# Two of eight channel blocks of a causal depthwise convolution on ScalarE and GpSimd, inside a decoder layer on one core

## The chip, the cores and the metric

One core of a Trainium2 chip runs the whole program. The metric is the device time of one execution in microseconds, as the median of several runs. Engines are named as in the profile: PE is TensorE, DVE is VectorE, ACT is ScalarE, POOL is GpSimd, SP is SyncE, which issues nearly all DMAs.

## The reference

One decoder layer for 256 tokens of width 2048, in float32. A matrix product with `w_in` gives columns for a convolution group and for an attention group. The part that matters here is the convolution group, with 1024 channels and 31 taps:

```python
a, g = jnp.split(conv_in, 2, axis=-1)
u = a * jax.nn.sigmoid(g)
u = causal_depthwise_conv(u, conv_w[l], conv_b[l])
u = jax.nn.silu(layernorm(u, conv_ln_g[l], conv_ln_b[l]))
```

The attention group (low-rank queries, keys and values, rotary key, causal softmax) runs between the convolution's input and the place where its result is used: both groups meet in the product with `w_out`. A SwiGLU feed-forward block of width 5632 follows, which is the larger part of the time and is not touched.

## The kernel before, in words

Every large matrix product is done in float16 with a split of both operands into an upper and a lower half: three matmuls on TensorE for one (lines 147 to 155). The weights come as float32 blocks of 128 x 2048 (four tiles of 128 x 512, or of 128 x 448 for the latent weights) through four stage buffers. `Weights.load` (L124) issues the DMA on SP's queue (L136), and `split` (L107) then makes the upper half on ScalarE (L108) and the lower half on VectorE (L109). The feed-forward weights go the same way through `Feed.split` (L690). There are eight buffers for each half, so the split can run ahead of TensorE by up to eight blocks.

The convolution works with channels in partitions: `upad` holds 8 channel blocks of 128 channels, each with 30 zeros and 256 tokens, and `cacc` the 8 sums of 128 x 256. The loop over `j` (L303) goes over four groups of `w_in` columns. Each gives two channel blocks, called a quarter: a matrix product, the GLU (tanh L312 and a scaled copy L314 on ScalarE, a product L316 on VectorE), a transpose on TensorE (L319) and a copy into `upad` (L320).

Each quarter puts 31 taps into the list `conv_todo`, and `pump(n)` takes the next n off it, in order. A tap of a quarter is one of three kinds (`conv_tap`, L279):

- tap 0: two ScalarE activations that write `cacc` with the bias (L284);
- a tap whose number is not a multiple of 4: two VectorE instructions of 128 x 256, one for each block, that multiply and add into `cacc` (L289);
- taps 4, 8, ..., 28: two ScalarE products into a buffer (L295), and one VectorE addition of 128 x 512 for both blocks (L297). The buffer is the space of `x_sb`, in 8 slots of 512 columns.

So a quarter is 46 instructions of L289 and 7 of L297 on VectorE, and 16 activations. The numbers in `PUMPS` (L36) say how many taps are given out at which place: after each of the four column groups, after each of the three groups of latent weights (`lat`, L365), after the rotary queries (`uqp`, L412), in the value projection (`v`, L422) and in each of the eight attention heads (`head`, L509). What is left would come before the LayerNorm (`ln_mean`, L528, called in the first part of the `w_out` product). The compiler's scheduler orders each engine's instructions by their place in the program and by when it takes them to be ready; on the chip each engine then runs its instructions in that order.

GpSimd has little to do: the power in the RMS norms (L207), and in each head a scaling of the probabilities (L481) and a sum of squares (L498, L500). The rope key (L374 to L386) is turned on VectorE (its last step is the copy L384) and transposed on TensorE (L385), in front of the rotary query products in TensorE's order.

Of the kernel before, what the change touches and what calls it, by code (L numbers as in the profile page):

```python
# [13 lines left out]
AF = mybir.ActivationFunctionType  # L14
ALU = mybir.AluOpType
# [3 lines left out]
S = 256  # L19
NTB = 2  # L20
D = 2048
KD = D // P
C = 1024
CB = C // P
TAPS = 31
# [6 lines left out]
KL = 512  # L32
FF = 5632
KF = FF // P
ACT_NUM, ACT_DEN = 1, 4
PUMPS = dict(conv=(3, 8, 13, 14), lat=(11, 16, 9), v=(1, 0), uqp=3, head=(2, 7, 4, 8, 4, 4, 9, 8))  # L36
NG = 22


# [9 lines left out]
W_S = 128.0  # L49
# [11 lines left out]
def hymba_layer(ctx: ExitStack, tc: tile.TileContext, x, xT, pos, inv_freq, g_pre, w_in, w_lat,  # L61
                q_norm, w_uqn, w_uqp, kv_norm, w_uk, w_uv, conv_w, conv_v, g_attn,
                w_out, g_post, g_ffn, w_gu, w_dn, g_ffo, out):
    nc = tc.nc
# [14 lines left out]
    def region(kb, shape, dtype=F32):  # L79

        n = int(np.prod(shape)) * (2 if dtype == F16 else 4) // 4
        a = int(kb * KB)
        v = arena[:, a : a + n]
        if dtype != F32:
            v = v.bitcast(dtype)
        names = "abcd"[: len(shape)]
        if len(shape) > 1:
            v = v.rearrange(f"p ({' '.join(names)}) -> p {' '.join(names)}", **dict(zip(names[:-1], shape[:-1])))
        return v
# [3 lines left out]
    def nm(base):  # L93
        uid[0] += 1
        return f"{base}_{uid[0]}"

    def acc_tile():
        return ps_acc.tile([P, 512], F32, tag="acc", name=nm("acc"))

    def tmp_tile():  # L100
        return ps_tmp.tile([P, 512], F32, tag="tmp", name=nm("tmp"))
# [5 lines left out]
    def split(hi, lo, src, scale):  # L107
        nc.scalar.activation(hi, src, AF.Copy, scale=scale)  # L108
        nc.vector.scalar_tensor_tensor(lo, src, scale, hi, op0=ALU.mult, op1=ALU.subtract)  # L109
# [6 lines left out]
    class Weights:  # L116
# [4 lines left out]
            self.kpb = max(1, 2048 // n)  # L121
            self.parts = []

        def load(self, src, scale, first=None, before=None):  # L124

            n = self.n
            per = self.kpb
            k0 = 0
            pieces = list(first or [])
            while k0 < self.kt:  # L130
                kk = pieces.pop(0) if pieces else per
                kk = min(kk, self.kt - k0)
                st = stage.tile([P, 2048], F32, tag="stage", name=nm("st"))
                if before is not None:
                    before(k0, k0 + kk)
                nc.sync.dma_start(st[:, : kk * n], src[:, k0 * n : (k0 + kk) * n])  # L136
                for j in range(0, kk, self.kpb):
                    w = min(self.kpb, kk - j) * n
                    hi = wsp.tile([P, 2048], F16, tag="whi", name=nm("whi"))
                    lo = wsp.tile([P, 2048], F16, tag="wlo", name=nm("wlo"))  # L140
                    split(hi[:, :w], lo[:, :w], st[:, j * n : j * n + w], scale)
                    for i in range(min(self.kpb, kk - j)):
                        self.parts.append((hi[:, i * n : (i + 1) * n], lo[:, i * n : (i + 1) * n]))
                k0 += kk
            return self

    def mm3(ps, x_of, wgt, tbs=(0, 1), k0=0, start=True, stop=True):

        for k in range(wgt.kt):
            wh, wl = wgt.parts[k]  # L150
            for p_ap, tb in zip(ps, tbs):
                xh, xl = x_of(k0 + k, tb)
                nc.tensor.matmul(p_ap, xh, wh, start=(start and k == 0), stop=False)  # L153
                nc.tensor.matmul(p_ap, xh, wl, start=False, stop=False)  # L154
                nc.tensor.matmul(p_ap, xl, wh, start=False, stop=(stop and k == wgt.kt - 1))  # L155
# [10 lines left out]
    def flat(h, l):  # L166

        return lambda k, tb: (h[:, k, TB[tb]], l[:, k, TB[tb]])
# [9 lines left out]
    x_sb = const.tile([P, NTB, D], F32, name="x_sb")  # L178
# [40 lines left out]
    wg1 = Weights(KD, 512).load(w_in[1], W_S, before=load_tokens)  # L219
# [4 lines left out]
    cw = region(26.5, (CB, TAPS))  # L224
    nc.sync.dma_start(cw, conv_w)
    cv = const.tile([P, 4, CB], F32, name="cv")
# [44 lines left out]
    upad = region(52, (CB, PAD + S))  # L271
    nc.gpsimd.memset(upad[:, :, 0:PAD], 0.0)
    cacc = region(61, (CB, S))

    conv_todo = []
    prod = x_sb.rearrange("p t (a c s) -> p (t a) c s", a=4, c=2)
    prod_n = [0]

    def conv_tap(quarter, k):  # L279

        cbs = range(2 * quarter, 2 * quarter + 2)
        if k == 0:
            for cb in cbs:
                nc.scalar.activation(cacc[:, cb, :], upad[:, cb, 0:S], AF.Identity, scale=cw[:, cb, 0:1],  # L284
                                     bias=cv[:, 0, cb : cb + 1])
            return
        if k % ACT_DEN >= ACT_NUM:
            for cb in cbs:
                nc.vector.scalar_tensor_tensor(cacc[:, cb, :], upad[:, cb, k : k + S], cw[:, cb, k : k + 1],  # L289
                                               cacc[:, cb, :], op0=ALU.mult, op1=ALU.add)  # L290
            return
        t = prod[:, prod_n[0] % 8]
        prod_n[0] += 1
        for i, cb in enumerate(cbs):
            nc.scalar.activation(t[:, i, :], upad[:, cb, k : k + S], AF.Copy, scale=cw[:, cb, k : k + 1])  # L295
        a = cacc[:, cbs[0] : cbs[-1] + 1, :]
        nc.vector.tensor_tensor(a, a, t, op=ALU.add)  # L297

    def pump(n):
        for _ in range(min(n, len(conv_todo))):  # L300
            conv_tap(*conv_todo.pop(0))

    for j in range(4):  # L303
        if j == 0:
            ps = ps0
        else:
            wgt = wg1 if j == 1 else Weights(KD, 512).load(w_in[j], W_S)
            ps = [acc_tile(), acc_tile()]
            mm3(ps, h_of, wgt)
        for tb in range(NTB):  # L310
            th = work.tile([P, 256], F32, tag="A", name=nm("th"), bufs=3)
            nc.scalar.activation(th, ps[tb][:, 256:512], AF.Tanh, scale=r_half[:, tb : tb + 1])  # L312
            av = work.tile([P, 256], F32, tag="B", name=nm("av"), bufs=3)
            nc.scalar.activation(av, ps[tb][:, 0:256], AF.Copy, scale=r_half[:, tb : tb + 1])  # L314
            u = work.tile([P, 256], F32, tag="C", name=nm("u"), bufs=2)
            nc.vector.scalar_tensor_tensor(u, th, 1.0, av, op0=ALU.add, op1=ALU.mult)  # L316
            tp = tmp_tile()
            for i in range(2):
                nc.tensor.transpose(tp[:, i * P : (i + 1) * P], u[:, i * P : (i + 1) * P], ident)  # L319
            nc.scalar.copy(upad[:, 2 * j : 2 * j + 2, PAD + tb * P : PAD + (tb + 1) * P],  # L320
                           tp[:, : 2 * P].rearrange("p (c t) -> p c t", c=2))
        conv_todo += [(j, k) for k in range(TAPS)]
        pump(PUMPS["conv"][j])


# [13 lines left out]
    def latent_norm(z, gb, n, hl, dst):  # L339
        for tb in range(NTB):  # L340
            ss = smalls()
            nc.scalar.activation(junk_tile(n), z[:, tb, :], AF.Square, accum_out=ss)
            r = rstd_of(ss, n)
            nc.vector.scalar_tensor_tensor(z[:, tb, :], z[:, tb, :], r, gb, op0=ALU.mult, op1=ALU.mult)
            split(hl[:, tb, 0, :], hl[:, tb, 1, :], z[:, tb, :], X_S)
            nc.sync.dma_start_transpose(dst.rearrange("p a k t -> p (a k) t")[:, :, TB[tb]],
                                        hl[:, tb].rearrange("p a n -> p (a n)"))
# [9 lines left out]
    for j in range(3):  # L357
        wgt = Weights(KD, LN).load(w_lat[j], W_S)
# [4 lines left out]
        if j == 1:  # L363
            latent_norm(z_q, g_q, QL, q_hl, qn)
        pump(PUMPS["lat"][j])  # L365

# [23 lines left out]
    wgt = Weights(QL // P, 512).load(w_uqp, W_S)  # L390
    ps = [acc_tile(), acc_tile()]
    mm3(ps, lat_of(qn), wgt)
    for tb in range(NTB):
# [17 lines left out]
        nc.scalar.copy(qpT[:, :, TB[tb]], tp.rearrange("p (i t) -> p i t", i=H // 2))  # L411
    pump(PUMPS["uqp"])  # L412


    v_sb = region(44, (NTB, H * P))
    for j in range(2):
        wgt = Weights(KL // P, 512).load(w_uv[j], W_S)
        ps = [acc_tile(), acc_tile()]
        mm3(ps, lat_of(kvn), wgt)
        for tb in range(NTB):  # L420
            nc.scalar.activation(v_sb[:, tb, j * 512 : (j + 1) * 512], ps[tb], AF.Copy, scale=U)
        pump(PUMPS["v"][j])  # L422

# [81 lines left out]
    for h in range(H):  # L505
        ss = scores(h)
        if h + 2 < H:
            project(h + 2)
        pump(PUMPS["head"][h])  # L509
        attend(h, ss)  # L510
# [54 lines left out]
    for j in range(4):  # L565
        wgt = Weights(CB, 512).load(w_out[4 + j], W_S)
        ps = [acc_tile(), acc_tile()]
        mm3(ps, flat(mx_h[:, CB:], mx_l[:, CB:]), wgt)
        for tb in range(NTB):
            nc.scalar.activation(mix[:, tb, j * 512 : (j + 1) * 512], ps[tb], AF.Copy, scale=r_a[:, tb : tb + 1])  # L570
        if j == 0:
            pump(len(conv_todo))
            ln_mean()
        elif j == 1:
            ln_var()
        elif j == 2:
            conv_norm()
            for tb in range(NTB):
                nc.sync.dma_start(x_sb[:, tb, :], x[:, tb, :])
# [408 lines left out]
```

## Time and profile before

| | us |
|---|---|
| median of 3 runs | 1000.91 |
| lowest and highest run | 1000.34, 1001.33 |
| the profiled execution's own time | 1001.55 |
| its span in the profile | 999.7 |
| TensorE busy in the span | 959.6 |
| VectorE busy | 876.3 |
| ScalarE busy | 578.1 |
| GpSimd busy | 33.6 |
| granted TensorE clock, share of full speed | 0.994 |

All views are of the profiled execution, whose time is its span and what lies around it. A busy share is the time in which at least one instruction of the engine runs; neighbouring instructions overlap by some 0.08 us, so the time that one takes of its engine's queue is read from the starts of a dense run. The convolution and the attention lie in the first 290 us.

### The profile page before, as it was taken

The numbers are of one execution on the slowest core, as the hardware profiler recorded it, in microseconds if no ns is written. First come the engines' busy times: TensorE is split into PE (matmuls) and PEld (weight loads), VectorE is DVE, ScalarE is ACT, GpSimd is POOL, SyncE is SP. The second block draws the span as 40 slices with busy tenths as digits, with TensorE's granted clock in tenths as the row PEclk, the third lists the DMA queues.
The fourth block names the chain that finished last, engine by engine and source line by source line (L and its number), as shares of the span: only waits on it lengthen the run. The fifth ranks groups of instructions, "written<-read, shape, count | busy, mean of one in ns | idle before, by whom it ended". The sixth has DMA issues, their size and how long they took to land.

```text
span 999.7 us, 11980 instructions
## 1 busy us (share of the span) xinstructions
PE 959.6 (96%) x4577; PEld 454.4 (45%) x4577; DVE 876.3 (88%) x1024; ACT 578.1 (58%) x632; POOL 33.6 (3%) x50
## 2 busy tenths in 40 slices
PE   6999997999899998999999999999999999999995
PEld 2444553775444443444444444444444444444442
DVE  6799999999967999989898997897996988899855
ACT  7796764664666555655656645654663565555521
POOL 0000000033100100000000000000000000000000
PEclk9999998999999999999999999999999999999998
DMA  8974656476654966776875874784686646645532
GB/s 340 346 262 126 243 197 192 154 247 211 211 210 118 325 167 197 256 278 197 320 214 178 317 236 155 272 288 156 220 309 234 218 185 246 238 175 220 210 127 85
DMA packets 84010, 221.95 MB, mean 222 GB/s; under 512 B 55792, under 2 KB 56432, under 8 KB 61424
## 3 DMA queue, kind: packets, MB, share of 16 engines
q1 hardware_dynamic: 83232, 220.26, 63.7%
q10 hardware_dynamic: 720, 0.93, 0.3%
q8 instruction: 36, 0.59, 0.2%
q14 instruction: 22, 0.18, 0.1%
HBM read 204.25 MB, written 4.19 MB: 209 GB/s over the span
## 4 chain that ended last, share of the span: by engine, by line
PE 60%; DVE 23%; issue 5%; ACT 4%; DMA 3%; POOL 1%; SPq 0%; DVEq 0%; POOLq 0%; ACTq 0%
PE acc L740 10%; PE acc L741 10%; PE acc L739 10%; PE tmp L741 6%; PE tmp L740 6%; PE tmp L739 6%; DVE wlo L695 6%; DVE arena L289 3%; DVE wlo L109 3%; DVE st L709 2%; PE acc L155 2%; PE acc L153 2%; PE acc L154 2%; DMA st<-in_w_gu 2%; POOL sm L207 1%
## 5 line engine op out<-in xcount | busy, mean ns | idle before, releaser
L694 ACT ACTIVATE whi<-st 128x2048 f16<-128x2048 f32 (+1 forms) x177 | 317.1, 1798 | 228.7 <-PE acc L741 77.6
L695 DVE SCALAR_TENSOR_TENSOR wlo<-st,whi 128x2048 f16<-128x2048 f32 (+1 forms) x177 | 375.2, 2150 | 52.9 <-ACT whi L694 52.5
L740 PE MATMUL acc<-wlo,arena 128*128 128x512 f16 x620 | 235.0, 379 | 4.7 <-DVE wlo L695 4.7
L739 PE MATMUL acc<-whi,arena 128*128 128x512 f16 x620 | 235.0, 379 | 2.5 <-DVE q L773 1.4
L741 PE MATMUL acc<-whi,arena 128*128 128x512 f16 x620 | 235.0, 379 | 0.0
L153 PE MATMUL acc<-whi,arena 128*128 128x512 f16 (+1 forms) x380 | 143.5, 378 | 5.5 <-ACT whi L108 5.5
L741 PEld LDWEIGHTS <-arena 128*128 128x128 f16 x951 | 93.0, 98 | 117.4 <-issue 5.6
L154 PE MATMUL acc<-wlo,arena 128*128 128x512 f16 (+1 forms) x380 | 143.4, 377 | 2.2 <-DVE wlo L109 2.0
L740 PEld LDWEIGHTS <-arena 128*128 128x128 f16 x951 | 93.0, 98 | 114.3 <-issue 2.4
L739 PEld LDWEIGHTS <-arena 128*128 128x128 f16 x951 | 93.0, 98 | 113.3 <-DVE a L796 1.2
L155 PE MATMUL acc<-whi,arena 128*128 128x512 f16 (+1 forms) x380 | 143.3, 378 | 0.0
L739 PE MATMUL tmp<-whi,arena 128*128 128x512 f16 x331 | 125.4, 379 | 0.0
L740 PE MATMUL tmp<-wlo,arena 128*128 128x512 f16 x331 | 125.4, 379 | 0.0
L741 PE MATMUL tmp<-whi,arena 128*128 128x512 f16 x331 | 125.4, 379 | 0.0
L109 DVE SCALAR_TENSOR_TENSOR wlo<-st,whi 128x2048 f16<-128x2048 f32 (+4 forms) x59 | 118.2, 2009 | 6.5 <-ACT whi L108 6.5
L709 DVE TENSOR_TENSOR st<-st 128x1024 f32<-128x1024 f32 x135 | 117.2, 868 | 4.1
L108 ACT ACTIVATE whi<-st 128x2048 f16<-128x2048 f32 (+4 forms) x59 | 98.5, 1677 | 34.4 <-PE acc L155 10.3
L289 DVE SCALAR_TENSOR_TENSOR arena<-arena 128x256 f32<-128x256 f32 x184 | 78.5, 488 | 0.0
L153 PEld LDWEIGHTS <-arena 128*128 128x128 f16 x380 | 37.8, 99 | 47.4 <-ACT arena L113 5.0
L155 PEld LDWEIGHTS <-arena 128*128 128x128 f16 x380 | 37.8, 99 | 44.8 <-issue 5.1
L154 PEld LDWEIGHTS <-arena 128*128 128x128 f16 x380 | 37.6, 99 | 42.3 <-issue 2.8
L295 ACT ACTIVATE x_sb<-arena 128x256 f32<-128x256 f32 x56 | 25.3, 506 | 10.1 <-DVE arena L297 10.1
(209 smaller groups left out, 667.9 us busy)
## 6 DMA issues: line engine op xcount, KB each, us to landing
st<-in_w_gu SPq DMA_DIRECT2D x88, 1024.0 KB, 5.5
st<-in_w_dn SPq DMA_DIRECT2D x44, 1024.0 KB, 5.0
st<-in_w_out SPq DMA_DIRECT2D x16, 1024.0 KB, 5.1
st<-in_w_in SPq DMA_DIRECT2D x14, 1024.0 KB, 9.2
st<-in_w_lat SPq DMA_DIRECT2D x12, 896.0 KB, 5.5
x_sb<-in_x SPq DMA_DIRECT2D x4, 1024.0 KB, 8.6
st<-in_w_uqn SPq DMA_DIRECT2D x4, 768.0 KB, 4.9
st<-in_w_uv SPq DMA_DIRECT2D x2, 1024.0 KB, 5.9
```

What stands on the lines that cost most here:

```text
L108: nc.scalar.activation(hi, src, AF.Copy, scale=scale)
L109: nc.vector.scalar_tensor_tensor(lo, src, scale, hi, op0=ALU.mult, op1=ALU.subtract)
L153: nc.tensor.matmul(p_ap, xh, wh, start=(start and k == 0), stop=False)
L154: nc.tensor.matmul(p_ap, xh, wl, start=False, stop=False)
L155: nc.tensor.matmul(p_ap, xl, wh, start=False, stop=(stop and k == wgt.kt - 1))
L289: nc.vector.scalar_tensor_tensor(cacc[:, cb, :], upad[:, cb, k : k + S], cw[:, cb, k : k + 1], cacc[:, cb, :], op0=ALU.mult, op1=ALU.add)
L694: self.chain("ACT", nc.scalar.activation(hi[:, :n], src, AF.Copy, scale=scale))
L695: self.chain("DVE", nc.vector.scalar_tensor_tensor(lo[:, :n], src, scale, hi[:, :n], op0=ALU.mult, op1=ALU.subtract))
L709: self.chain("DVE", nc.vector.tensor_tensor(d, p, m, op=ALU.add))
L739: nc.tensor.matmul(ps, ah, bh, start=key not in self.begun, stop=False)
L740: nc.tensor.matmul(ps, ah, bl, start=False, stop=False)
L741: nc.tensor.matmul(ps, al, bh, start=False, stop=last)
```

## The change

Channel blocks 1 and 3 (the second block of quarter 0 and of quarter 1) are taken out of VectorE's work. All their taps are made of a ScalarE product of 128 x 256 and a GpSimd addition into `cacc`; tap 0 stays an activation. They have a list of their own, `pool_todo`, with 62 entries. It is given out by `pump_pool`: 8 entries after each column group, and 4 behind each weight block's split of the third and the fourth column group (through the new argument `behind` of `Weights.load`). Blocks 0 and 2, now alone in their quarter's taps, do all 30 taps with L289's kind of instruction. Quarters 2 and 3 keep the three kinds of taps. The buffer for the products becomes 16 slots of 256 columns, and a pair takes two that lie together. `PUMPS` is changed: 62 taps in the place of 38 are given out in the convolution stage, and 29 in the place of 46 in the heads. The number of products, sums and taps in the result is the same.

```diff
-ACT_NUM, ACT_DEN = 1, 4
-PUMPS = dict(conv=(3, 8, 13, 14), lat=(11, 16, 9), v=(1, 0), uqp=3, head=(2, 7, 4, 8, 4, 4, 9, 8))
+ACT_DEN = 4
+PUMPS = dict(conv=(8, 16, 20, 18), lat=(10, 12, 8), v=(1, 0), uqp=2, head=(2, 4, 3, 5, 3, 3, 5, 4))
+POOL_CB = (1, 3)
+POOL_PUMPS = dict(conv=(8, 8, 8, 8), w_in=(0, 0, 4, 4))
...
                     split(hi[:, :w], lo[:, :w], st[:, j * n : j * n + w], scale)
+                    if behind is not None:
+                        behind()
...
-    prod = x_sb.rearrange("p t (a c s) -> p (t a) c s", a=4, c=2)
+    pool_todo = []
+    prod = x_sb.rearrange("p t (a s) -> p (t a) s", s=S)
...
+    def product(t, cb, k):
+        nc.scalar.activation(t, upad[:, cb, k : k + S], AF.Copy, scale=cw[:, cb, k : k + 1])
+
+    def next_prod(n):
+        prod_n[0] += -prod_n[0] % n + n
+        a = (prod_n[0] - n) % 16
+        return prod[:, a : a + n, :]
+
+    def conv_tap(cbs, k):
+
         if k == 0:
             for cb in cbs:
...
+                first_tap(cb)
+        elif len(cbs) == 1 or k % ACT_DEN:
             for cb in cbs:
                 nc.vector.scalar_tensor_tensor(cacc[:, cb, :], upad[:, cb, k : k + S], cw[:, cb, k : k + 1],
                                                cacc[:, cb, :], op0=ALU.mult, op1=ALU.add)
...
+    def pump_pool(n):
+
+        for _ in range(min(n, len(pool_todo))):
+            cb, k = pool_todo.pop(0)
+            if k == 0:
+                first_tap(cb)
+                continue
+            t = next_prod(1)[:, 0, :]
+            product(t, cb, k)
+            nc.gpsimd.tensor_tensor(cacc[:, cb, :], cacc[:, cb, :], t, op=ALU.add)
...
-            wgt = wg1 if j == 1 else Weights(KD, 512).load(w_in[j], W_S)
+            wgt = wg1 if j == 1 else Weights(KD, 512).load(
+                w_in[j], W_S, behind=lambda: pump_pool(POOL_PUMPS["w_in"][j]))
...
-        conv_todo += [(j, k) for k in range(TAPS)]
+        conv_todo += [([cb for cb in (2 * j, 2 * j + 1) if cb not in POOL_CB], k) for k in range(TAPS)]
+        pool_todo += [(cb, k) for cb in POOL_CB if cb // 2 == j for k in range(TAPS)]
+        pump_pool(POOL_PUMPS["conv"][j])
         pump(PUMPS["conv"][j])
...
         if j == 0:
+            pump_pool(len(pool_todo))
             pump(len(conv_todo))
```

## Rows read from the trace of the kernel before

**Rows 1.** The page, part 1: busy us (share of the span) and instructions.

```profile
PE 959.6 (96%) x4577; PEld 454.4 (45%) x4577; DVE 876.3 (88%) x1024; ACT 578.1 (58%) x632; POOL 33.6 (3%) x50
```

**Rows 2.** Windows: start:end, length, busy us (instructions) of PE, PEld, DVE, ACT, POOL; clock, DMA, GB/s.

```profile
46.90:96.60 49.70, 48.20 (x226) 21.99 (x225) 48.40 (x78) 40.56 (x62) 0.00 (x0) 1.00 0.55 186
96.60:156.40 59.80, 58.93 (x310) 30.02 (x307) 58.92 (x86) 37.67 (x48) 1.64 (x2) 1.00 0.68 226
156.40:162.60 6.20, 0.00 (x0) 0.00 (x0) 4.76 (x19) 5.32 (x10) 0.58 (x2) 0.93 0.60 221
162.60:170.00 7.40, 7.37 (x22) 3.08 (x23) 6.96 (x14) 3.07 (x5) 0.58 (x1) 0.60 0.44 83
200.00:249.40 49.40, 46.30 (x287) 31.60 (x286) 46.88 (x93) 29.49 (x62) 16.26 (x21) 1.00 0.68 229
249.40:290.00 40.60, 37.35 (x177) 17.22 (x175) 33.56 (x29) 29.75 (x34) 4.32 (x3) 1.00 0.54 186
```

**Rows 3.** Timeline, DVE: dense taps and the splits of the latent weights.

```profile
81.82 3.26 DVE L289 SCALAR_TENSOR_TENSOR arena<-arena 128x256 f32<-128x256 f32 x8
84.99 0.69 DVE L297 TENSOR_TENSOR arena<-arena,x_sb 128x512 f32<-128x512 f32 x1
85.59 3.26 DVE L289 SCALAR_TENSOR_TENSOR arena<-arena 128x256 f32<-128x256 f32 x8
91.94 2.02 DVE L109 SCALAR_TENSOR_TENSOR wlo<-st,whi 128x1792 f16<-128x1792 f32 x1
133.36 2.02 DVE L109 SCALAR_TENSOR_TENSOR wlo<-st,whi 128x1792 f16<-128x1792 f32 x1
```

**Rows 4.** Timeline, PE and ACT: start, us, instruction, count, idle time before it and its releaser.

```profile
96.65 0.47 ACT L312 ACTIVATE th<-acc,r_half 128x256 f32<-128x256 f32 x1 [3.67 <-PE acc L155]
157.28 1.48 ACT L108 ACTIVATE whi<-st 128x1536 f16<-128x1536 f32 x1 [1.88 <-DMA st<-in_w_uqn]
162.63 0.48 PE L385 MATMUL tmp<-ident,kp 128*128 128x128 f32 x1 [6.24 <-DVE kp L384]
```

**Rows 5.** Timeline, DVE: two steps that each read what the one before wrote.

```profile
44.23 0.23 DVE L245 TENSOR_SCALAR arena<-arena 128x128 f32<-128x128 f32 x1
44.50 0.23 DVE L246 TENSOR_SCALAR arena<-arena 128x128 f32<-128x128 f32 x1
```

**Rows 6.** Timeline, POOL and DVE in the heads: additions of 128x256 beside DVE work.

```profile
232.65 0.75 POOL L500 TENSOR_TENSOR arena<-arena,sq 128x256 f32<-128x256 f32 x1 [4.34 <-ACT sq L496]
232.72 2.82 DVE L109 SCALAR_TENSOR_TENSOR wlo<-st,whi 128x2048 f16<-128x2048 f32 x1
...
240.23 1.81 POOL L500 TENSOR_TENSOR arena<-arena,sq 128x256 f32<-128x256 f32 x1 [2.66 <-ACT sq L496]
239.17 2.28 DVE L109 SCALAR_TENSOR_TENSOR wlo<-st,whi 128x2048 f16<-128x2048 f32 x1
...
245.98 0.82 POOL L500 TENSOR_TENSOR arena<-arena,sq 128x256 f32<-128x256 f32 x1 [2.70 <-ACT sq L496]
245.35 2.92 DVE L289 SCALAR_TENSOR_TENSOR arena<-arena 128x256 f32<-128x256 f32 x6
```

**Rows 7.** Groups of DVE instructions from 46.11 to 94.0 us.

```profile
L289 DVE SCALAR_TENSOR_TENSOR arena<-arena 128x256 f32<-128x256 f32 x53 | 21.9, 482 | 0.0
L297 DVE TENSOR_TENSOR arena<-arena,x_sb 128x512 f32<-128x512 f32 x8 | 5.5, 690 | 0.1
```

**Rows 8.** Groups of ACT instructions from 46.88 to 96.6 us.

```profile
L295 ACT ACTIVATE x_sb<-arena 128x256 f32<-128x256 f32 x32 | 14.4, 511 | 5.5 <-DVE arena L297 5.5
L284 ACT ACTIVATE arena<-arena,cv 128x256 f32<-128x256 f32 x6 | 3.4, 596 | 0.1
```

**Rows 9.** Timeline, ACT: a run of products, and the first latent weights cast.

```profile
58.64 2.13 ACT L295 ACTIVATE x_sb<-arena 128x256 f32<-128x256 f32 x5
72.82 1.70 ACT L108 ACTIVATE whi<-st 128x1792 f16<-128x1792 f32 x1
```

More of the change, by code (lines that the diff above doesn't have):

```diff
@@ L122, in __init__, with load @@
             self.parts = []
-        def load(self, src, scale, first=None, before=None):
+        def load(self, src, scale, first=None, before=None, behind=None):
             n = self.n
@@ L275, in hymba_layer, with first_tap @@
     conv_todo = []
-    prod = x_sb.rearrange("p t (a c s) -> p (t a) c s", a=4, c=2)
+    pool_todo = []
+    prod = x_sb.rearrange("p t (a s) -> p (t a) s", s=S)
     prod_n = [0]
-    def conv_tap(quarter, k):
-        cbs = range(2 * quarter, 2 * quarter + 2)
+    def first_tap(cb):
+        nc.scalar.activation(cacc[:, cb, :], upad[:, cb, 0:S], AF.Identity, scale=cw[:, cb, 0:1],
+                             bias=cv[:, 0, cb : cb + 1])
+    def product(t, cb, k):
[5 more added lines that the diff above has]
+    def conv_tap(cbs, k):
         if k == 0:
             for cb in cbs:
[L284 to L287, printed above, removed]
+                first_tap(cb)
+        elif len(cbs) == 1 or k % ACT_DEN:
             for cb in cbs:
@@ L290, in conv_tap @@
                                                cacc[:, cb, :], op0=ALU.mult, op1=ALU.add)
[L291 to L297, printed above, removed]
+        else:
+            t = next_prod(2)
+            for i, cb in enumerate(cbs):
+                product(t[:, i, :], cb, k)
+            a = cacc[:, cbs[0] : cbs[-1] + 1, :]
+            nc.vector.tensor_tensor(a, a, t, op=ALU.add)
+    def pump_pool(n):
[7 more added lines that the diff above has]
+            nc.gpsimd.tensor_tensor(cacc[:, cb, :], cacc[:, cb, :], t, op=ALU.add)
     def pump(n):
```

## The prediction

> **What bounds the kernel now.** I read the busy shares first: TensorE is busy for 959.6 of 999.7 us, so all that can be gained is its idle time, and VectorE comes next with 88% [rows 1]. The reader is to see there that the free engine is GpSimd (3%), and that VectorE has little room. The profiled execution took 1001.55 us (span 999.7 us plus 1.85 us around it); that is 0.64 us above the median of the runs, 1000.91 us. The changes below are taken from the profiled execution and added to the median. A difference under 0.2%, 2 us, could not be told from no change.
>
> Then the stretches around the change [rows 2]. From 46.90 us, where the first taps can start, to 96.60 us, where the last w_in group ends on TensorE, VectorE is busy for 48.40 of 49.70 us; in the latent stage, up to 156.40 us, for 58.92 of 59.80 us. TensorE is full there too (48.20 and 58.93 us): it never waits for weights, but only because the split that VectorE makes (the lower half, L109) arrives just in time. The first split of the latent weights starts at 91.94 us and ends at 93.96 us [rows 3]; TensorE finishes the group before it at 96.6 us, since the tanh at 96.65 us had waited for it [rows 4]. So the lead at the end of the convolution stage is 2.6 us. The last latent split ends at 135.4 us [rows 3] for a group that TensorE works on until 156.4 us, so the lead then grows.
>
> TensorE's idle time that the change can reach: 1.5 us in the first stretch, 6.2 us from 156.40 us, where it waits for the rope key [rows 2, 4], after which it runs at a granted 0.60, a mixture of its two levels, for 7.4 us; and 3.1 us in the heads and 3.25 us around the LayerNorm [rows 2]. 1.9 us of the 6.2 us are ScalarE's: it stood at a weight cast whose DMA was late, with the copy of the latents behind it [rows 4].
>
> **Step 1, VectorE's own work.** Dense taps start every 0.396 us (eight from 81.82 us, the next instruction at 84.99 us), and an addition of 512 columns takes 0.60 us of the queue (84.99 to 85.59 us) [rows 3]. Quarters 0 and 1 cost 2 x (46 taps + 7 additions) = 92 x 0.396 + 14 x 0.60 = 44.8 us; after the change 2 x 30 taps, 60 x 0.396 = 23.8 us. Relief at best 21.1 us. But the 60 taps form one chain for one block, each reading what the last wrote. The trace shows such pairs starting 0.04 us after the end of the one before (0.23 us long, 0.27 us apart) [rows 5]; for a tap of 0.48 us that would be 0.52 us, 60 x 0.52 = 31.2 us. Between 23.8 and 31.2 us I take 23.8, because where a GpSimd sum stands between two taps this wait lies inside the sum.
>
> **Step 2, 60 sums on GpSimd.** The nearest row is the sum of squares in the heads, the same shape: 0.75 us long where nothing held it [rows 6]. What matters is what it does to VectorE. Beside it a split took 2.82 us where one alone takes 2.28 (+0.54), and six taps took 2.92 us where 5 x 0.396 + 0.48 = 2.46 is usual (+0.46) [rows 6]. When VectorE was first, the sum took 1.81 us and VectorE lost nothing [rows 6]. So they take turns: a sum costs VectorE 0.50 us where its queue is dense (lower bound 0, as in the last case; upper bound the whole 0.75 us), and a split holds the sum up.
>
> The Trainium skill, "SBUF — State Buffer", section "Who interferes with whom", speaks against the change: a VectorE instruction with two SBUF inputs and a GpSimd instruction that reads SBUF exclude each other, and the second blocks until the first has finished. By that rule each sum would cost its whole 0.75 us, 15 us more over 60 sums (1031 us in the place of 1016); the rows show about two thirds of it.
>
> Taps, splits and the GLU product all have two SBUF inputs, and VectorE is dense there [rows 2], so 60 x 0.50 = 30 us come in and 21.1 us go out: VectorE is worse off by 9 us in all, and by more early on.
>
> **Step 3, where it falls.** From 46.11 to 94.0 us VectorE does 53 taps and 8 additions [rows 7]: 53 x 0.396 + 8 x 0.60 = 25.8 us. After the change all 60 chained taps are given out ahead of the latent weights (8 + 16 + 20 + 18 turns, less the two first taps), 23.8 us, with their sums. I take 50 of the 60 sums as done by then (25 us), because a sum every 0.90 us (0.396 + 0.50), held up by eight splits of 2.2 us, is not quite through by then. 23.8 + 25 - 25.8 = 23.0 us later; less the lead of 2.6 us, **TensorE starts the latent group 20.4 us later**. It is full from there on and can't make it up.
>
> From there to the rope key VectorE gets 10 sums (5 us) and loses 6 us (lat 30 turns for 36, uqp 2 for 3: 12 taps and 2 additions, 4.8 + 1.2 us): nothing, and the lead grows as now. The late DMA behind the rope key's gap should no longer be late, since the split that frees its buffer is ahead of TensorE: -1.9 us. In the heads 29 turns are left for 46: 24 taps and 4 additions fewer, 11.9 us of VectorE. TensorE's idle time there and in the LayerNorm is 6.35 us; I give half of it back, -3.2 us, the rest being latency through ScalarE and GpSimd.
>
> **Step 4, edits taken at nothing.** ScalarE: quarters 0 and 1 need 64 activations for 32, all in the convolution stage. Today 38 lie there, some drawn forward [rows 8]; 26 more at 0.405 us (five in 2.13 us, the last 0.505 us long) [rows 9] are 10.5 us for 9.1 us of free time [rows 2]. The cover is the lead of its weight casts: the first latent one is done at 74.5 us [rows 9], 22 us early. If that cover went, TensorE would wait for ScalarE. The products go to 16 slots of 256 columns in the place of 8 of 512: the same room, but a product behind a late sum now waits in ScalarE's queue, with casts and tanh behind it. No DMA is added or moved past another; SP's queue only follows the buffers. GpSimd has no other work in the convolution stage [rows 2].
>
> **Sum.** +20.4 + 0 - 1.9 - 3.2 = +15.3 us; 1000.9 + 15.3 = **1016 us**. Its own range is 1008 (35 sums in front at 0.46 us: 9 us less) to 1028 (60 sums in front, +5, and the chained 0.52 us, +7.4).
>
> **Rivals.**
> - *The sums hold VectorE for their full length.* 60 x 0.25 us more: 1031 us; a TensorE that waits at every block would also run at the lower level, as after its 6.2 us of idling [rows 2]. For: the rule named above. Against: the two stretched rows. 0.14.
> - *ScalarE becomes the bound.* VectorE is stretched by no more than its relief, but a product waits for a slot with weight casts behind it, and the 8.7 us by which 44 more activations in program order (17.8 us) exceed the free 9.1 us come out on TensorE: 1010 us. Against it speaks the 22 us lead. 0.11.
> - *Nothing shows.* A stretch of 0.15 us, the sums lying mostly in VectorE's pauses: 23.8 + 9 - 25.8 - 2.6 = 4.4 us, and the -5.1 us of step 3: 1000 us. 0.09.
> - *Faster: the relief is real.* GpSimd's sums run in the waits of VectorE's new single chain (0.12 us each) and behind the splits, where one took 1.81 us and cost VectorE nothing [rows 6]. Then VectorE keeps up, the DMA wait of 1.9 us goes, the late GLU transposes save 1, and two thirds of the 6.35 us in the heads and LayerNorm go: -7 us, 994 us. It decides from a stretch under 0.1 us per sum. For it: the chain leaves gaps that today's pairs don't. Against it: 0.12 us is shorter than a sum, and two of the three rows show the stretch. 0.18.
>
> **How the numbers follow.** The forecast has 0.48, so slower by over 0.2% has 0.48 + 0.14 + 0.11 = 0.73, within 0.2% 0.09, faster 0.18. The forecast is the likeliest case, 1016 us. The range goes from 994, leaving out half of the faster case, to 1036 us (all 60 sums in front at 0.75 us: 23.8 + 45 - 25.8 - 2.6 - 5.1 = +35.3), which leaves out a little of the first rival.
>
> **What would show it.** Right: taps and splits with a second length some 0.5 us above the first between 50 and 120 us; GpSimd sums of 0.7 to 2.5 us, some 60 x 0.9 us busy; VectorE full up to about 120 us, the first latent split ending at about 117 us; TensorE waiting for L109 from the third w_in group on, and a lower granted clock there. Step 3 is wrong if the first latent split ends before 100 us, step 4 if TensorE waits for L108. Taps still 0.48 us long beside the sums, and a TensorE as full as today up to 156 us, would make the prediction wrong as a whole.

## The result, and the profile after

The changed kernel takes 1035.58 us (median of 4 runs, 1034.93 to 1038.07); the kernel before took 1001.08 us beside it. The ratio is 1.0351, with a 95% interval of 1.0333 to 1.0368: 34.5 us slower, where 15.3 us had been forecast. The profiled execution took 1038.07 us, with a span of 1036.2 us, 36.5 us more than the span before.

The page of the changed kernel, part 1, answers to [rows 1]:

```profile
PE 973.8 (94%) x4577; PEld 459.5 (44%) x4577; DVE 882.3 (85%) x978; ACT 592.6 (57%) x664; POOL 90.9 (9%) x110
```

GpSimd's busy time rose by 57 us and ScalarE's by 15 us, but VectorE's did not fall: it is 6 us higher, with 46 instructions fewer. The dense taps show why. The timeline of VectorE in the changed kernel (start, us, instruction, count; L305 is the tap, L113 the split), against [rows 3]; then the group of its taps from 46.11 us to the first latent split, against [rows 7] (count, busy us, mean ns); then GpSimd's sums (the same, and ns min/median/max, first and last start):

```profile
57.83 10.66 DVE L305 SCALAR_TENSOR_TENSOR arena<-arena 128x256 f32<-128x256 f32 x12
68.41 2.81 DVE L113 SCALAR_TENSOR_TENSOR wlo<-st,whi 128x2048 f16<-128x2048 f32 x1
...
116.82 2.01 DVE L113 SCALAR_TENSOR_TENSOR wlo<-st,whi 128x1792 f16<-128x1792 f32 x1
```

```profile
L305 DVE SCALAR_TENSOR_TENSOR arena<-arena 128x256 f32<-128x256 f32 x51 | 42.3, 834 | 3.7 <-ACT arena L287 2.4
```

```profile
L323 POOL TENSOR_TENSOR arena<-arena,x_sb 128x256 f32<-128x256 f32 x60 | 58.6, 978 | 21.7 <-ACT x_sb L291 17.3
L323 POOL TENSOR_TENSOR arena<-arena,x_sb x60: 725/788/2772, 49.0 to 115.8; 128x256 f32<-128x256 f32 x60
```

Twelve taps take 10.66 us, 0.89 us each, and a split 2.81 us in the place of 2.28. The 51 taps in front of the first latent split take 834 ns on average, where 53 took 482. Where the sums are over, this split has its old 2.01 us; it ends at 118.8 us, 24.9 us later than before the change. Now TensorE: its first latent product in the kernel before and in the changed kernel, then the windows up to there, before and changed (columns as in [rows 2]), then the changed kernel in pieces:

```profile
97.09 0.35 PE L153 MATMUL acc<-whi,arena 128*128 128x448 f16 x1
121.11 0.35 PE L159 MATMUL acc<-whi,arena 128*128 128x448 f16 x1
```

```profile
46.90:97.01 50.11, 48.61 (x228) 22.18 (x227) 48.81 (x78) 40.93 (x63) 0.00 (x0) 1.00 0.55 188
46.98:121.11 74.13, 57.71 (x228) 24.57 (x227) 70.37 (x69) 54.28 (x96) 58.63 (x60) 0.84 0.39 129
```

```profile
46.90:60.00 13.10, 9.98 (x43) 4.33 (x41) 10.46 (x13) 10.97 (x26) 9.84 (x13) 0.88 0.52 189
60.00:70.00 10.00, 5.52 (x17) 2.04 (x16) 9.68 (x11) 10.00 (x16) 9.14 (x12) 0.82 0.00 1
70.00:80.00 10.00, 8.72 (x35) 3.75 (x35) 9.93 (x9) 10.00 (x20) 9.53 (x8) 0.83 0.54 177
80.00:90.00 10.00, 8.05 (x38) 3.50 (x37) 9.75 (x12) 4.30 (x10) 9.21 (x11) 1.00 0.39 138
90.00:100.00 10.00, 4.40 (x11) 1.64 (x11) 9.89 (x10) 1.89 (x2) 6.24 (x6) 0.55 0.34 100
100.00:110.00 10.00, 10.00 (x38) 4.32 (x37) 9.82 (x9) 9.87 (x19) 8.53 (x8) 0.77 0.50 177
110.00:121.10 11.10, 11.10 (x53) 5.00 (x51) 10.89 (x12) 7.24 (x9) 6.14 (x7) 1.00 0.37 110
...
127.00:133.00 6.00, 5.99 (x21) 3.09 (x22) 6.00 (x12) 5.97 (x8) 0.00 (x0) 0.59 0.48 185
...
185.40:188.00 2.60, 0.04 (x1) 0.00 (x0) 2.16 (x14) 0.33 (x3) 0.63 (x1) 1.00 0.97 344
188.00:195.40 7.40, 6.86 (x32) 3.15 (x33) 6.92 (x19) 4.45 (x6) 0.76 (x1) 1.00 0.55 170
```

TensorE starts the latent group 24.0 us later. With the same 228 instructions in the two windows it is idle for 16.4 us (1.5 us before) and busy for 57.7 us (48.6 before): 14.9 us more idling, and 9.1 us more for the same products at a lower clock. The granted clock is between 0.55 and 0.88 in five of the seven pieces up to 121.1 us, so TensorE was at its lower level for part of each. But the first latent split is 24.9 us late and TensorE 24.0 us, so idling and slow clock together did not add to VectorE's lateness; the slow work seems to have filled time in which TensorE would else have waited for splits.

What it waited for in the changed kernel (total us, times, longest):

```profile
PE acc L160 <- DVE wlo L113: 13.5, 4, 5.8
PE tmp L346 <- DVE u L343: 9.2, 4, 4.0
PE acc L159 <- ACT whi L112: 6.2, 2, 5.5
PE tmp L515 <- POOL ss L510: 5.4, 3, 4.2
PE tmp L414 <- DVE kp L413: 3.1, 2, 2.6
```

L160 and L346 wait for VectorE (splits, GLU product), as forecast, with one exception. The longest wait of L346, 4.0 us, comes after TensorE has begun with the latent weights, and its chain runs through a DMA and ScalarE (changed kernel; L140 issues the DMA, L112 is ScalarE's weight cast):

```profile
118.86 0.33 SPq L140 DMA_DIRECT2D st<-in_w_lat  x1
...
123.47 1.70 ACT L112 ACTIVATE whi<-st 128x1792 f16<-128x1792 f32 x1 [3.72 <-DMA st<-in_w_lat]
125.07 0.46 ACT L339 ACTIVATE th<-acc,r_half 128x256 f32<-128x256 f32 x1
...
127.01 0.48 PE L346 MATMUL tmp<-ident,u 128*128 128x128 f32 x1 [4.03 <-DVE u L343]
```

The DMA starts at 118.86 us, when the late split (116.82 + 2.01 us) has freed its stage buffer. ScalarE waits 3.7 us for it with a weight cast, and the tanh stands behind that cast, though its products were done at about 121.3 us. The GLU, and TensorE's transposes, come after that; TensorE then works for six microseconds at a granted 0.59.

The longest wait at the rope key (L414) is 2.65 us in the place of 6.24 [rows 4], and the clock behind it did not drop. The wait L515 for the softmax is new. Two more rows: the tanh of the column groups and, for both kernels, the copy of each head's queries (duration min/median/max, first and last start):

```profile
L339 ACT ACTIVATE th<-acc,r_half x8: 457/476/477, 36.8 to 125.8; 128x256 f32<-128x256 f32 x8
```

```profile
L472 ACT ACTIVATE qT<-tmp x8: 360/376/386, 208.4 to 265.1; 128x256 f32<-128x256 f32 x8
```

```profile
L443 ACT ACTIVATE qT<-tmp x8: 363/370/384, 184.2 to 229.4; 128x256 f32<-128x256 f32 x8
```

The second tanh of the last column group starts at 125.8 us (97.4 before): +28.4 us, of which some 4 us are ScalarE's wait just shown. The first query copy is 24.2 us later, the last one 35.7 us: the heads, 45.2 us before, take 56.7 us. So there are two losses, one of about 25 us up to the heads and one of 11.5 us within them. VectorE, TensorE and the windows there show the second (changed kernel; L558 is the first reduction of the LayerNorm, L506 the reciprocal of a head's softmax sum, L515 the transpose that needs it):

```profile
238.12 3.71 DVE L558 TENSOR_REDUCE arena<-arena 128x256 f32<-128x2048 f32 x1
241.74 0.15 DVE L506 RECIPROCAL sm<-sm 128x2 f32<-128x2 f32 x1
```

```profile
244.38 0.33 PE L515 MATMUL tmp<-ident,ss 128*128 128x128 f32 x1 [4.17 <-POOL ss L510]
```

```profile
235.00:245.00 10.00, 5.71 (x42) 4.48 (x42) 9.09 (x14) 5.88 (x10) 3.57 (x3) 0.98 0.56 236
245.00:255.00 10.00, 10.00 (x30) 6.07 (x31) 3.41 (x7) 1.23 (x3) 0.72 (x1) 0.51 0.63 210
```

Since the taps now end in the heads, the reduction's input is ready early, and it stands in VectorE's queue in front of a reciprocal. The reciprocal comes only behind its 3.7 us, TensorE waits 4.2 us, and then works for ten microseconds at a granted 0.51, the lower of its two levels (1.2 GHz).

### The profile page after: what moved, and what is told of

The parts are those of the page before. It is cut to its first block, busy times and chain, and to the rows that moved or that the text cites. A ratio compares the mean times of both kernels' runs of the same rounds, so it can differ in the third digit from the quotient of the medians.

```text
span 1036.2 us, 12095 instructions
## 1 busy us (share of the span) xinstructions
PE 973.8 (94%) x4577; PEld 459.5 (44%) x4577; DVE 882.3 (85%) x978; ACT 592.6 (57%) x664; POOL 90.9 (9%) x110
## 4 chain that ended last, share of the span: by engine, by line
PE 57%; DVE 23%; issue 5%; ACT 5%; DMA 2%; POOL 2%; SPq 0%; DVEq 0%; POOLq 0%; ACTq 0%
PE acc L770 10%; PE acc L771 10%; PE acc L769 10%; PE tmp L771 6%; PE tmp L769 6%; PE tmp L770 6%; DVE wlo L725 6%; DVE arena L305 4%; DVE wlo L113 4%; PE acc L159 2%; PE acc L160 2%; PE acc L161 2%; DVE st L739 2%; DMA st<-in_w_gu 2%; ACT x_sb L291 1%
## 5 line engine op out<-in xcount | busy, mean ns | idle before, releaser
L160 PE MATMUL acc<-wlo,arena 128*128 128x512 f16 (+1 forms) x380 | 147.0, 387 | 13.7 <-DVE wlo L113 13.5
L159 PE MATMUL acc<-whi,arena 128*128 128x512 f16 (+1 forms) x380 | 146.4, 386 | 6.4 <-ACT whi L112 6.2
L161 PE MATMUL acc<-whi,arena 128*128 128x512 f16 (+1 forms) x380 | 146.3, 385 | 0.0
L113 DVE SCALAR_TENSOR_TENSOR wlo<-st,whi 128x2048 f16<-128x2048 f32 (+4 forms) x59 | 121.6, 2071 | 12.7 <-ACT whi L112 12.7
L112 ACT ACTIVATE whi<-st 128x2048 f16<-128x2048 f32 (+4 forms) x59 | 98.5, 1677 | 27.6 <-PE acc L161 11.6
L305 DVE SCALAR_TENSOR_TENSOR arena<-arena 128x256 f32<-128x256 f32 x152 | 85.2, 601 | 3.9 <-ACT arena L287 2.4
L161 PEld LDWEIGHTS <-arena 128*128 128x128 f16 x380 | 38.4, 101 | 58.9 <-issue 20.4
L323 POOL TENSOR_TENSOR arena<-arena,x_sb 128x256 f32<-128x256 f32 x60 | 58.6, 978 | 21.7 <-ACT x_sb L291 17.3
L160 PEld LDWEIGHTS <-arena 128*128 128x128 f16 x380 | 38.3, 101 | 44.7 <-issue 6.3
```

## The experiments

All are timed beside the kernel before. "Latent" is the start of TensorE's first product with latent weights, "tanh" the last start of the tanh, "heads" the time from the first to the last query copy, all of the profiled execution. The executions are apart by up to 1.8 us from early on (first tanh at 35.0 to 36.8 us), so differences below that in the columns "latent" and "tanh" say nothing.

| run | us | ratio, 95% interval | latent | tanh | heads |
|---|---|---|---|---|---|
| kernel before | 1000.8 to 1001.3 | 1 | 97.1 | 97.4 | 45.2 |
| changed kernel | 1035.58 | 1.0351 (1.0333 to 1.0368) | 121.1 | 125.8 | 56.7 |
| sums as memsets | 1017.36 | 1.0160 (1.0144 to 1.0176) | 101.2 | 103.2 | 58.7 |
| sums on VectorE | 1018.08 | 1.0176 (1.0155 to 1.0197) | 109.0 | 109.3 | 50.0 |
| reduction behind the heads | 1026.91 | 1.0255 (1.0238 to 1.0272) | 118.3 | 124.3 | 46.7 |
| tap schedule of before | 1021.35 | 1.0202 (1.0187 to 1.0218) | 115.6 | 116.3 | 48.6 |
| memsets, reduction behind | 1006.06 | 1.0052 (1.0037 to 1.0067) | 101.4 | 103.1 | 47.3 |
| copies, reduction behind | 1009.88 | 1.0090 (1.0071 to 1.0108) | 105.0 | 107.9 | 46.9 |
| before, rope key after the rotary queries | 1001.42 | 1.0002 (0.9991 to 1.0014) | 96.8 | 97.1 | 45.2 |
| before, rope key after the values | 1016.74 | 1.0147 (1.0121 to 1.0174) | 96.8 | 97.1 | 53.4 |

**Sums as memsets.** A GpSimd instruction that only writes, in the place of each sum:

```diff
-            nc.gpsimd.tensor_tensor(cacc[:, cb, :], cacc[:, cb, :], t, op=ALU.add)
+            nc.gpsimd.memset(t, 0.0)
```

> The changed kernel with each of the 60 GpSimd sums replaced by a GpSimd memset of the product's slot, which reads no SBUF; the order of VectorE, ScalarE and TensorE is unchanged. Channel blocks 1 and 3 are left without their sums. Theory 1 (GpSimd's sums and VectorE's instructions with two SBUF inputs take turns, 0.49 us for a sum): taps start every 0.40 to 0.52 us in the place of 0.89, splits take 2.28 us in the place of 2.81, the tanh of the last column group comes at 97 to 103 us in the place of 125.1, and the whole is 1006 to 1014 us. Rival (the order: products in front of the weight casts, taps in front of the splits): TensorE still waits for L113 near 65 us, that tanh comes after 110 us, the whole is over 1020 us. Rival (any GpSimd instruction holds VectorE): the taps stay near 0.9 us, the whole near 1035 us.

VectorE's timeline in this run, in which nearly half of the memsets lie beside a split:

```profile
54.78 6.21 DVE L305 SCALAR_TENSOR_TENSOR arena<-arena 128x256 f32<-128x256 f32 x12
60.90 2.29 DVE L113 SCALAR_TENSOR_TENSOR wlo<-st,whi 128x2048 f16<-128x2048 f32 x1
```

Twelve taps now take 6.21 us, 0.52 us each, and the split 2.29 us. The latent group starts 19.9 us sooner than in the changed kernel, and the tanh comes at 103.2 us, 22.6 us sooner. This part is theory 1's, and the order of the instructions is not the cause: it is the same here on VectorE, ScalarE and TensorE. TensorE's waits for splits fall from 13.5 to 4.5 us. The total of 1017 us misses the expected 1006 to 1014 us, since the heads stay long (58.7 us); that loss has another cause.

**Sums on VectorE.**

```diff
-            nc.gpsimd.tensor_tensor(cacc[:, cb, :], cacc[:, cb, :], t, op=ALU.add)
+            nc.vector.tensor_tensor(cacc[:, cb, :], cacc[:, cb, :], t, op=ALU.add)
```

> The changed kernel with the same 60 sums of 128x256 issued on VectorE. Theory 1: a sum costs VectorE about 0.34 us as an instruction of its own (as two 128x256 additions start 0.34 us apart in the rotary queries) and 0.49 us as GpSimd's, so the kernel gets faster without GpSimd: 1024 to 1031 us. Rival (GpSimd does relieve VectorE, and the loss is ScalarE's products): 60 more VectorE instructions make it slower than 1036 us, by up to 20 us.

VectorE's timeline in this run (L323 is the sum):

```profile
59.05 0.42 DVE L323 TENSOR_TENSOR arena<-arena,x_sb 128x256 f32<-128x256 f32 x1
59.38 0.49 DVE L305 SCALAR_TENSOR_TENSOR arena<-arena 128x256 f32<-128x256 f32 x1
59.78 0.42 DVE L323 TENSOR_TENSOR arena<-arena,x_sb 128x256 f32<-128x256 f32 x1
```

A tap and a sum together take VectorE 0.73 us (59.05 to 59.78), less than a tap beside a GpSimd sum (0.89 us). The rival falls: VectorE is better off doing the sum itself. The run is 17.5 us faster than the changed kernel, more than the 5 to 12 us expected: the latent group starts 12.1 us sooner and the heads are 6.7 us shorter. How much of it is the price of the sums alone is not shown, since the scheduler also put VectorE's and ScalarE's instructions in another order here.

**Reduction behind the heads.** One edge that orders, without a wait:

```diff
-        nc.vector.tensor_reduce(csum, ...)
+        red = nc.vector.tensor_reduce(csum, ...)
+        tc.add_manual_dep(red.ins, head_end[0].ins.name, NO_SYNC, reason="mean behind the heads")
```

> The changed kernel with one more ordering edge: the LayerNorm's first reduction (3.7 us on VectorE) stays behind the last head. Theory 2 (since the taps end sooner, this reduction was drawn in front of a softmax reciprocal; TensorE waited 4.2 us and then ran 10 us at a granted 0.51): the heads get 7 to 10 us shorter, the convolution stage is unchanged (tanh of the last column group at 125 us), the whole is 1026 to 1029 us. Rival (the heads wait for the softmax chain anyway, with fewer taps to do): 1033 us or more.

The query copies in this run:

```profile
L472 ACT ACTIVATE qT<-tmp x8: 360/374/384, 206.9 to 253.6; 128x256 f32<-128x256 f32 x8
```

The heads take 46.7 us, 10 us less than in the changed kernel and 1.5 us more than before; the convolution stage stays late (tanh at 124.3 us). The whole is 8.7 us faster, inside the expected range. Theory 2 holds: in VectorE's order only the reduction has moved.

**Tap schedule of before.** `PUMPS` as in the kernel before, the sums unchanged.

> The changed kernel with the tap schedule of the kernel before (38 turns in the convolution stage, 46 in the heads); the sums stay on GpSimd and where they are. Theory 1: the stage has 36 taps and its sums, 14.3 + 29.4 us, in the place of 25.8 us before, so the latent stage starts some 15 us later than before the change (about 112 us), the reduction is not drawn forward, and the whole is 1012 to 1021 us. Rival (ScalarE's products and GpSimd's sums alone set the convolution stage): that stage is as late as in the changed kernel (125 us), the whole is over 1026 us.

```profile
L339 ACT ACTIVATE th<-acc,r_half x8: 456/473/475, 36.2 to 116.3; 128x256 f32<-128x256 f32 x8
```

That row is the tanh in this run: 18.9 us later than before the change; the latent group starts 18.5 us later, where 15 us had been expected, and the total, 1021.35 us, is just above the range. The rival falls. Giving the taps out sooner accounts for 14 of the 34.5 us: the latent group starts 5.5 us sooner than in the changed kernel and the heads are 8.1 us shorter. The rest of the change, with the old schedule, still costs 20 us.

**Memsets, and the reduction behind the heads.** Both edits together.

> The run with the reduction held behind the heads, with the 60 GpSimd sums replaced by memsets that read no SBUF (blocks 1 and 3 are left without their sums); all orders as in that run. If the turns of GpSimd and VectorE (theory 1) and the drawn reduction (theory 2) are the whole loss, then what is left is the single chain of 60 taps, 0.52 in the place of 0.40 us, 7 us of VectorE less the lead of 2.6 us: 1002 to 1008 us, and a heads stage within 2 us of the kernel before. Rival (ScalarE's 26 more products cost something of their own): 1010 us or more.

```profile
L472 ACT ACTIVATE qT<-tmp x8: 360/374/383, 187.4 to 234.7; 128x256 f32<-128x256 f32 x8
```

The heads take 47.3 us and the whole 1006.06 us, in the expected range. The four kernels with and without each edit (1035.6, 1017.4, 1026.9 and 1006.1 us) show that the memsets give back 18 and 21 us and the edge 9 and 11 us, each without and with the other edit: two losses that nearly add up, 29.5 of the 34.5 us. With both taken out, the changed kernel is still 5 us slower than the one before, though GpSimd now costs VectorE nothing: with this tap schedule the relief that the change aims at brings no gain. Memsets with the tap schedule of before were not run, so a gain there is not ruled out. The chain of single taps, 0.52 us apart in the place of 0.40, would explain a lateness of this size; it was not varied by itself.

**Copies, and the reduction behind the heads.** GpSimd reads one operand:

```diff
-            nc.gpsimd.tensor_tensor(cacc[:, cb, :], cacc[:, cb, :], t, op=ALU.add)
+            nc.gpsimd.tensor_copy(cacc[:, cb, :], t)
```

> As the run before, but each sum replaced by a GpSimd copy of the product into cacc: one SBUF input in the place of two (blocks 1 and 3 hold one product, not the sum). Theory 1, read as any GpSimd read of SBUF against VectorE's second input, with a hold that grows with what is read: a tap beside a copy starts every 0.6 to 0.75 us (0.52 alone, 0.89 beside a sum), the whole is 1009 to 1019 us. Rival (only a GpSimd instruction with two inputs collides): 0.52 us a tap, 1002 to 1008 us, as with the memsets. Rival (a whole turn is lost whatever GpSimd reads): 0.85 us or more, 1023 to 1029 us.

VectorE's timeline and GpSimd's copies in this run (ns min/median/max):

```profile
56.20 6.50 DVE L305 SCALAR_TENSOR_TENSOR arena<-arena 128x256 f32<-128x256 f32 x12
62.62 2.48 DVE L113 SCALAR_TENSOR_TENSOR wlo<-st,whi 128x2048 f16<-128x2048 f32 x1
```

```profile
L323 POOL COPY arena<-x_sb x60: 400/472/2341, 48.9 to 97.7; 128x256 f32<-128x256 f32 x60
```

A split takes 2.48 us, 0.20 us more than alone. The twelve taps take 0.54 us each, less than the expected 0.6 to 0.75 us; that most of the hold lies in the chain's own pause would explain it, but is not shown. GpSimd is held too: most copies take 0.47 us in the place of the 0.40 us that the heads' own copy (L527) takes in the same run, and seven that start beside a split take 1.8 to 2.3 us. The total lies in the range of theory 1, and the second rival's 1023 us is far off. The first rival's 1002 to 1008 us is missed by less; against it speak the split, and 3.8 us more than with the memsets in kernels that are else in the same order: one operand costs less than two, but more than none.

**Rope key moved, in the kernel before.** The largest gap of the trace before is the one at the rope key, and two runs try to close it: the block L371 to L386 moved to after L412 (first run), or to after L422 (second).

> The kernel before, with the rope key (its turn on VectorE, its transpose and copy) moved behind the rotary queries in program order, so that TensorE has the rotary query products to do where it now waits 6.2 us for the key and then runs at a granted 0.60. If that wait was only the order: 992 to 998 us. Rival (the normed kv latents, which the value projection needs, come no earlier, and the wait moves there): 999 to 1003 us.

> As the run before, with the rope key behind the value projection too. Same two theories: 992 to 998 us, or 999 to 1003 us where the wait moves to the value projection.

TensorE's longest wait in the first of these runs:

```profile
PE acc L153 <- DMA arena<-arena: 8.0, 1, 8.0
```

The rival holds: TensorE now waits 8.0 us in the value projection, for the DMA transpose of the normed latents, and the time is the same. With the key behind the values too, the order of the heads changes, TensorE waits 11.0 us in them for the softmax (1.0 us before), and the time is 1.5% longer. No version here beats the kernel before.

## Why the prediction was right or wrong

The direction was right, and the mechanism of step 2 as well. A tap beside a sum was put at 0.90 us and took 0.89; the 60 sums at 60 x 0.9 us, and GpSimd was busy with them for 58.6 us (0.79 us for most, and 2.66 to 2.77 us for six that stood beside a split); the first latent split was to end at about 117 us and ended at 118.8. The two thirds of a sum that the rows gave as its price were the better choice: a split is 0.53 us longer. The rule of the Trainium skill ("SBUF — State Buffer", section "Who interferes with whom") has the right sign. Its clause that a GpSimd instruction which only writes doesn't collide with VectorE's second input agrees with the memsets (a split of 2.29 us beside them). That the second instruction blocks for the whole of the first is not what the trace shows: 0.53 us of a sum of 0.75 us, and the measurement decides.

The size was wrong, by more than a factor of two. The forecast adds +20.4, 0, -1.9 and -3.2 us; the trace has +24.0 us at the first latent product, +5.0 from there to the gap at the rope key, -3.6 in that gap, -1.3 from there to the first query copy, +11.5 in the heads and +0.8 behind them, together the 36.5 us of the two profiled executions. The largest failure is the sign of the last term.

**Step 3, "I give half of it back, -3.2 us".** The heads lost 11.5 us instead. I had counted VectorE's load there, which did fall (from the first query copy on, 27 taps and 4 additions in the place of 58 and 9), and not asked what the earlier end of the taps would release into the queue. It released the LayerNorm's reduction, into the middle of the softmax chain: TensorE waited 4.2 us and ran ten microseconds at half its clock. Held back, it gave 8.7 us again.

**Step 3, "From there to the rope key ... nothing".** It was +5.0 us: 3.2 us more of waiting for the last GLU transposes (4.03 us for 0.85), and 1.9 us more of work behind it, with a granted clock of 0.59 at first. I had taken the lead for safe from the first latent product on. But the last GLU, which TensorE needs a little later, had its tanh behind a weight cast on ScalarE, and the cast's DMA waited for a buffer that VectorE's late split freed.

**Step 3, "TensorE starts the latent group 20.4 us later".** It was 24.0 us, a smaller miss. VectorE was 24.9 us late in the place of 23.0: 51 taps and all 60 sums stood in front, not 60 and 50, and at the prices of steps 1 and 2 that is 51 x 0.396 + 60 x 0.50 - 25.8 = 24.4 us. The lead that I subtracted whole, 2.6 us (3.1 us by the first latent product), was not used up: 2.3 us of it were left (118.83 to 121.11 us), since TensorE was held up before by the splits of the w_in weights (waits of 5.8 us from 65.5 us and 5.5 us from 88.0 us).

The third term, -1.9 us at the rope key, had the right sign; the gap became 3.6 us shorter.

**Step 4** held in part: the casts on ScalarE were not TensorE's bound directly (6.2 us of waits for them in the whole trace, 5.5 before). But "SP's queue only follows the buffers" was left at nothing, and here a late buffer made a late DMA, with a cast and the last tanh behind it. **Step 1** took 0.396 us for a tap where a sum stands beside it; tap and hold together, 0.89 us, came out, though the trace can't tell this from 0.52 us with a shorter hold. The 0.52 us named as its upper end is what the chain takes without sums.

The rival "faster" falls: in no run of the changed kernel was there a gain, and even with sums that cost VectorE nothing this schedule takes 1006 us. TensorE was nearly full before the change, so a relief of VectorE could only have worked on the 14 us of idle time that the windows showed.

## What to carry to other kernels

Before moving elementwise work from VectorE to GpSimd, look at whether VectorE's queue is dense with instructions that read two SBUF operands there: what counts is the price that the moved instruction takes of VectorE's queue (0.5 us for a sum here) against the one that it saves (21.1 us over 60 sums, 0.35 us each). A lateness can come back by another way: here a late split freed a buffer late, the DMA into it was late, and a tanh stood behind the cast that waited for it. And when work ends sooner, look at what its successor will now stand in front of: a scheduler that goes by readiness puts it there, and 3.7 us at the wrong place cost 8.7 us here.

## What the runs showed of the hardware

The hold that GpSimd puts on VectorE grew with the operands that it reads: a memset of 128x256 cost a split of 2048 columns nothing (2.29 us), a copy 0.20 us, a sum 0.53 us. GpSimd's own length is a poor guide to it: the sum takes 0.73 to 0.75 us where nothing holds it, the copy 0.40 us, the memset 0.31 us. The hold goes both ways: six sums that started 0.6 to 0.8 us after a split took 2.66 to 2.77 us and ended some 0.6 us behind it. And two waits of TensorE, of 4.2 us in the heads and 4.0 us at the last GLU, were followed by ten microseconds at a granted 0.51 and six at 0.59, while the gap of 2.65 us at the rope key was followed by 7.4 us at 1.00.
